# Queueing VectorE's comparisons of the next group ahead of the low half of the weights, in a fused transformer kernel

## The chip, the cores and the metric

The kernel runs on one core of one Trainium2 chip. The metric is the device time of one execution in microseconds (us). Three runs of the kernel before took 1719.59, 1720.41 and 1721.41 us.

## What is computed

The reference is three layers in a row on 256 tokens of width 1024: an attention layer and a gated convolution layer, each with a SwiGLU, and a third layer with a mixer, a cross attention and a mixture of 16384 small experts (PEER). Only that last part matters here. For each token and each of 8 heads it picks 16 experts; expert e = 128 i + j has one row of `u` and one of `v`:

```
s = jnp.einsum('thpc,hpnc->thpn', q, subkeys)
s_top, i_top = lax.top_k(s, PEER_TOPK)
...
experts = jnp.take_along_axis(cand_idx..., pos, axis=-1)
gates = jax.nn.softmax(best, axis=-1)
...
act = jax.nn.gelu(jnp.einsum('cd,ced->ce', xb, u[eb]), approximate=False) * gb
y = jnp.einsum('ce,ced->cd', act, v[eb])
```

The kernel does not gather rows of `u` and `v`. It computes gelu(u x) for all 16384 experts and all 256 tokens, multiplies by a gate that is zero for every expert that a token did not pick, and multiplies by all of `v`.

## The kernel before

**Weights.** A weight stream (class `Stream`) brings all weights in chunks of 1 MB into two raw buffers; SyncE (SP) issues the loads (L215). Each chunk is used in two half chunks. For each of them ScalarE makes a rounded high half `wh` (L231), and VectorE a low half `wl` = raw - wh (L243), and TensorE multiplies three times: high by high, high by low, low by high (L329, L330, L331). There are three buffers each of `wh` and `wl`. The stream works two halves ahead (`look` is 2): the call `w(k)`, which hands out one half, first queues the high and low half of the half chunk two further on. The load that refills a raw buffer is queued behind the second low half of its old chunk.

**The u stage.** The loop `for c in range(NC)` runs over 64 chunks of `u`, with `k` = 0 and 1 for the halves. `proj_stat` gives one half's product u x in 24 matmuls of 256 columns; `gelu` (L1592, L1595) writes it into the tile `big`, which has a column for each of 128 second keys j and 256 tokens, on 128 partitions of first keys i.

**The gates.** For tokens 0 to 127 the gates are written one by one into DRAM by GpSimd (L1491, L1492), loaded back in the v stage (L1534) and multiplied in by GpSimd (L1539). For tokens 128 to 255 they are made in the second part of the u stage, in 32 groups of 4 tokens, which I call the one-hot phase. It is counted in halves e = 2c + k - 91. In half 0 TensorE transposes the selections and ScalarE copies them to `ET` (`hot_T`, L1563, L1564). For group g:

- `hot_make(g)`, on VectorE: one comparison of 512 columns gives the one-hot rows `oi` of the first keys (L1571), four of 128 columns the rows `oj` of the second keys times the gate (L1574). `oi` and `oj` have two slots, g modulo 2.
- `hot_mm(g, J)`: four small matmuls on TensorE give the gates of four tokens in a bank `acc` (L1581); VectorE multiplies them into the columns of `big` that gelu has already written (L1584), and ScalarE copies the rest (L1585) to columns that gelu will meet later. There gelu goes through a buffer `gx`, and a multiply of VectorE or, from group 13 on, of GpSimd (L1596) brings it into `big`; `gated()` queues that one.

In half e the program makes group e-1 and multiplies group e-2.

**What sets the order.** Every engine takes its instructions in the order in which the program writes them; semaphores are placed by the framework from the tiles that are read and written. In half e the code calls, before the change: `w(k)`, the gelu of the chunk before, `proj_stat`, `hot_make(e - 1)`, `gated()`, `hot_mm(e - 2)`.

**The v stage.** Behind the u stage, chunks of `v` are multiplied with `big`, split into high and low parts by `asplit` (ScalarE L361, VectorE L362).

Of the kernel before, what the change touches and what calls it, by code (L numbers as in the profile page):

```python
# [32 lines left out]
HOT0 = 91  # L33
# [230 lines left out]
def body(ctx, tc, I, O):  # L264
# [11 lines left out]
    def bank():  # L276
        return mm.tile([128, 512], F32, name="mm")
# [57 lines left out]
    def proj_stat(ps, w, k, x):  # L335
        w = w(k)
        if FRESH.pop(id(x[0]), None):
            for kt in range(KT):
                a = kt * 128
                for i in range(2):  # L340
                    P.matmul(ps, w[i][:, a:a + 128], x[0][:, kt, :], start=kt + i == 0, stop=False)
            for kt in range(KT):
                a = kt * 128
                P.matmul(ps, w[0][:, a:a + 128], x[1][:, kt, :], start=False, stop=kt == KT - 1)
            return
        for kt in range(KT):
            a = kt * 128
            mm3(ps, w[0][:, a:a + 128], w[1][:, a:a + 128], x[0][:, kt, :], x[1][:, kt, :], kt == 0, kt == KT - 1)
# [582 lines left out]
    for i in range(12):  # L931
        w = W.get(("cv", i))
        for k in range(2):
            c, j = cseq[2 * i + k]
# [294 lines left out]
    for hs in range(8):  # L1229
# [4 lines left out]
        i, k = divmod(hs - 2, 2)  # L1234
# [203 lines left out]
    def pump(b):  # L1438
        credit[0] = min(credit[0] + b, 3.0)
        while RU and credit[0] >= RU[0][0]:  # L1440
            c, f = RU.pop(0)
            credit[0] -= c
            f()
# [92 lines left out]
    def g_mul(c):  # L1536
        if c < NE // 2:
            b = big[:, 2 * c:2 * c + 2, 0:128]
            G.tensor_tensor(b, b, GT.pop(c), op=OP.mult)  # L1539
# [7 lines left out]
    def asplit(j):  # L1547
        if j < NE:
            h, l = AV[j if j < 2 else 2 + j % 4]
            split_to(h, l, big[:, j, :])  # L1550
            AB[j] = (h, l)
# [8 lines left out]
    def hot_T():  # L1560
        ps = bank()
        for i, a in enumerate((0, 1, 3)):
            P.transpose(ps[:, i * 128:i * 128 + 128], slots[:, a, 128:256], ident)  # L1563
        A.activation(ET, ps[:, :384].rearrange("p (a b) -> p a b", a=3), AF.Copy)  # L1564

    def hot_make(g):
        ts = slice(124 - 4 * g, 128 - 4 * g)
        oi, oj = OI[:, g % 2], OJ[:, g % 2]
        io = iota[:, None, :].to_broadcast([128, 4, 128])

        V.tensor_tensor(oi, io, ET[:, 0, ts, None].to_broadcast([128, 4, 128]), op=OP.is_equal)  # L1571
        for i in range(4):
            t = 124 - 4 * g + i
            V.tensor_scalar(oj[:, i, :], iota, ET[:, 1, t:t + 1], ET[:, 2, t:t + 1], op0=OP.is_equal, op1=OP.mult)  # L1574
        HOT[g] = (oi, oj)

    def hot_mm(g, J):
        oi, oj = HOT.pop(g)
        ps = accp.tile([128, 512], F32, name=("acc00", "acc01", "acc10", "acc11")[g % 4])
        for i in range(4):  # L1580
            P.matmul(ps[:, i * 128:i * 128 + 128], oi[:, i, :], oj[:, i, :], start=True, stop=True)  # L1581
        pv = ps.rearrange("p (t j) -> p j t", t=4)
        b = big[:, :, 252 - 4 * g:256 - 4 * g]
        V.tensor_tensor(b[:, :J, :], b[:, :J, :], pv[:, :J, :], op=OP.mult)  # L1584
        A.activation(b[:, J:, :], pv[:, J:, :], AF.Copy)  # L1585
        HB[0] = g + 1

    def gelu(c, ps):
        n = 4 * HB[0]
        p3 = ps.rearrange("p (a b) -> p a b", a=2)  # L1590
        b = big[:, 2 * c:2 * c + 2, :]
        A.activation(b[:, :, :S - n], p3[:, :, :S - n], AF.Gelu)  # L1592
        if n:
            x = bx.tile([128, 2, 128], F32, name="gx", bufs=1)
            A.activation(x[:, :, :n], p3[:, :, S - n:], AF.Gelu)  # L1595
            late.append(lambda: (V if n <= 48 else G).tensor_tensor(b[:, :, S - n:], b[:, :, S - n:], x[:, :, :n], op=OP.mult))  # L1596
# [3 lines left out]
    def gated():  # L1600
        while late:
            late.pop(0)()

    for c in range(NC):
        w = W.get(("u", c))
        ps = bank()
        if 2 * c + 2 >= NE - 32:
            assert not RU
        for k in range(2):
            w(k)  # L1610
            while pend:
                pend.pop(0)()
            if c == NC - 1 and k == 1:
                g_mul(0)
                as0 = bx.tile([128, 4, 256], F32R, name="oi", bufs=1)
                AV += [(as0[:, 0, :], as0[:, 1, :]), (as0[:, 2, :], as0[:, 3, :])]
                asplit(0)
                asplit(1)
            proj_stat(ps[:, k * 256:k * 256 + 256], w, k, xT)
            pump(CRED1)  # L1620
            e = 2 * c + k - HOT0
            if e >= 0:
                assert not RU
            if e == 0:
                hot_T()
            if 1 <= e < 34:
                if e < 33:
                    hot_make(e - 1)
                gated()
                if e > 1:  # L1630
                    hot_mm(e - 2, 2 * c)
            gated()
        pend.append(lambda c=c, ps=ps: gelu(c, ps))
    pend.pop(0)()
    gated()
# [77 lines left out]
```

## Time and profile before

| what | value |
|---|---|
| median of three runs | 1720.41 us |
| the profiled execution | 1723.32 us |
| its span | 1721.5 us |
| granted TensorE clock, mean | 0.992 |
| TensorE (PE) busy | 1656.5 us, 96% |
| VectorE (DVE) busy | 1175.8 us, 68% |
| ScalarE (ACT) busy | 815.0 us, 47% |
| GpSimd (POOL) busy | 483.2 us, 28% |
| DMA, mean | 184 GB/s |

Times within the profile are in us from the start of the span. An engine's busy share is an average over all stages. A row of the timeline gives a start, a duration, the engine, the line of the code, what it writes and reads, and in brackets how long the engine sat idle before it and which instruction ended that. Matmuls are pipelined, so a row of TensorE lasts longer than the step to the next one; the pace is read from the starts.

### The profile page before, as it was taken

The page shows a single profiled execution, that of the slowest core. Times are in us where ns is not written, and L with a number is a line of the kernel's source. Part 1 is how long each engine was busy: PE and PEld are TensorE (multiplying, and loading weights), DVE is VectorE, ACT ScalarE, POOL GpSimd, SP SyncE. Part 2 cuts the span into 40 slices and gives each one's busy share as a digit, 9 for nine tenths or more (in the row PEclk, how much of TensorE's full clock was granted, in tenths as well). Part 3 has the DMA queues.
Part 4 walks back from the last instruction along what each step waited for, and adds up shares of the span by engine and source line. Part 5 has one row for each costly group of instructions (what it writes and reads, how often), then busy time and mean ns, then how long its engine had stood idle before and what let it go on. Part 6 is the DMA issues. An engine that isn't in the chain of part 4 may idle for free.

```text
span 1721.5 us, 27583 instructions
## 1 busy us (share of the span) xinstructions
PE 1656.5 (96%) x11013; PEld 1505.5 (87%) x11013; DVE 1175.8 (68%) x2069; ACT 815.0 (47%) x1260; POOL 483.2 (28%) x446
## 2 busy tenths in 40 slices
PE   8899999999999998998999999999888999999997
PEld 7888999899999977887989999999887888888886
DVE  5897554667654564776558889888777666666665
ACT  5564444434444444564445545445332444444544
POOL 0542000200200022203037887788501211111111
PEclk9999999999999999999999999999999999999999
DMA  7346776455555545434355676766433566666664
GB/s 272 137 140 231 256 237 234 172 208 200 207 182 196 177 166 192 164 104 145 122 193 167 178 196 176 193 181 188 100 121 101 188 219 206 209 219 209 207 217 171
DMA packets 80416, 317.48 MB, mean 184 GB/s; under 512 B 25120, under 2 KB 41760, under 8 KB 45344
## 3 DMA queue, kind: packets, MB, share of 16 engines
q1 hardware_dynamic: 59120, 304.38, 51.7%
q0 software_dynamic: 20736, 10.56, 4.1%
q8 instruction: 86, 1.41, 0.3%
q10 hardware_dynamic: 432, 0.79, 0.1%
q14 instruction: 42, 0.34, 0.1%
HBM read 303.04 MB, written 10.55 MB: 182 GB/s over the span
## 4 chain that ended last, share of the span: by engine, by line
PE 47%; DVE 8%; issue 3%; ACT 3%; POOL 1%; DMA 1%; POOLq 0%; DVEq 0%; ACTq 0%
PE acc L331 8%; PE acc L330 7%; PE acc L329 7%; PE mm L329 7%; PE mm L331 7%; PE mm L330 7%; ACT wh L231 2%; DVE oj L1574 2%; DVE oi L1571 1%; DVE big L1584 1%; DVE wl L243 1%; DMA xTl<-mTl 1%; DVE qkm L1062 1%; POOL wl L243 0%; PE mm L1460 0%
## 5 line engine op out<-in xcount | busy, mean ns | idle before, releaser
L243 DVE TENSOR_TENSOR wl<-raw,wh 128x1024 fp32r<-128x1024 f32 (+1 forms) x511 | 631.5, 1254 | 301.6 <-ACT wh L231 300.3
L231 ACT ACTIVATE wh<-raw 128x1024 fp32r<-128x1024 f32 (+1 forms) x537 | 552.6, 1053 | 377.4 <-PE acc L331 181.7
L329 PE MATMUL mm<-xTh,wh 128*128 128x256 f32 x2328 | 660.2, 284 | 1.1 <-DVE mTl L378 1.1
L331 PE MATMUL mm<-xTh,wl 128*128 128x256 f32 x2328 | 655.8, 282 | 1.8 <-DVE wl L243 1.5
L330 PE MATMUL mm<-xTl,wh 128*128 128x256 f32 x2328 | 655.3, 281 | 0.0
L329 PEld LDWEIGHTS mm<-xTh,wh 128*128 128x128 f32 x2328 | 441.6, 190 | 3.9 <-DVE mTl L378 1.5
L331 PEld LDWEIGHTS mm<-xTh,wl 128*128 128x128 f32 x2328 | 441.3, 190 | 2.7 <-DVE wl L243 1.9
L330 PEld LDWEIGHTS mm<-xTl,wh 128*128 128x128 f32 x2328 | 441.5, 190 | 0.9
L1492 POOL DMA_INDIRECT gd<-slots,idx x128 | 259.9, 2030 | 68.9 <-issue 32.3
L329 PE MATMUL acc<-wh,xTh 128*128 128x512 f32 x632 | 249.7, 395 | 0.0
L330 PE MATMUL acc<-wl,xTh 128*128 128x512 f32 x632 | 249.2, 394 | 0.2 <-DVE wl L243 0.2
L243 POOL TENSOR_TENSOR wl<-raw,wh 128x1024 fp32r<-128x1024 f32 x26 | 64.6, 2491 | 566.8 <-ACT wh L231 565.2
L331 PE MATMUL acc<-wh,xTh 128*128 128x512 f32 x504 | 201.1, 399 | 0.0
L330 PEld LDWEIGHTS acc<-wl,xTh 128*128 128x128 f32 x632 | 119.1, 188 | 30.2 <-DVE wl L243 0.8
L329 PEld LDWEIGHTS acc<-wh,xTh 128*128 128x128 f32 x632 | 119.0, 188 | 28.7 <-issue 0.7
L1539 POOL TENSOR_TENSOR big<-big,oj 128x256 f32<-128x256 f32 x64 | 57.5, 898 | 290.3 <-DMA oj<-gd 290.3
L331 PEld LDWEIGHTS acc<-wh,xTh 128*128 128x128 f32 x504 | 94.6, 188 | 21.7
L880 DVE TENSOR_TENSOR sil<-sil,mm 128x256 f32<-128x256 f32 x44 | 18.5, 421 | 102.7 <-ACT sil L879 102.7
L879 ACT ACTIVATE sil<-mm 128x256 f32<-128x256 f32 x44 | 16.9, 385 | 148.4 <-PE mm L331 148.4
L362 DVE TENSOR_TENSOR xTh<-big,xTh 128x256 fp32r<-128x256 f32 x126 | 79.4, 630 | 0.0
L1491 POOL MEMSET spacer<- 1x1 f32 x128 | 78.9, 616 | 0.0
L330 PE MATMUL acc<-wl,hTh 128*128 128x512 f32 x176 | 69.6, 395 | 0.0
(388 smaller groups left out, 1844.2 us busy)
## 6 DMA issues: line engine op xcount, KB each, us to landing
raw<-in_ws_dram SPq DMA_DIRECT2D x131, 1024.0 KB, 5.1
raw<-in_us_dram SPq DMA_DIRECT2D x64, 1024.0 KB, 5.1
raw<-in_vs_dram SPq DMA_DIRECT2D x64, 1024.0 KB, 4.9
gd<-zt SPq DMA_DIRECT2D x32, 256.0 KB, 6.9
raw<-in_pq_dram SPq DMA_DIRECT2D x8, 1024.0 KB, 4.9
oj<-gd SPq DMA_DIRECT2D x64, 128.0 KB, 4.8
gb<-in_vec_dram POOLq DMA_DIRECT2D x12, 512.0 KB, 7.1
gd<-slots,idx POOLq DMA_INDIRECT x128, 4.0
```

The lines of the kernel that those rows point to most:

```text
L231: self.nc.scalar.activation(h[:, s], self.R[i][:, k * HW:(k + 1) * HW][:, s], AF.Copy)
L243: self.sub[k].tensor_tensor(l[:, s], self.R[i][:, k * HW:(k + 1) * HW][:, s], h.bitcast(F32)[:, s], op=OP.subtract)
L329: P.matmul(ps, lh, rh, start=first, stop=False)
L330: P.matmul(ps, lh, rl, start=False, stop=False)
L331: P.matmul(ps, ll, rh, start=False, stop=last)
L362: V.tensor_tensor(l, src, h.bitcast(F32), op=OP.subtract)
L880: V.tensor_tensor(s, s, pg[:, 256:], op=OP.mult)
L1062: V.scalar_tensor_tensor(y[:, a, :], pad[:, a, j:j + 256], cols[:, 24 + 4 * ft + j:25 + 4 * ft + j], y[:, a, :], op0=OP.mult, op1=OP.add)
L1491: G.memset(spacer, 0.0)
L1492: d = G.indirect_dma_start(out=gd, out_offset=bass.IndirectOffsetOnAxis(ap=idx[:, h, k:k + 1], axis=0), in_=gate[:, 0, h, k:k + 1], in_off ...
L1539: G.tensor_tensor(b, b, GT.pop(c), op=OP.mult)
L1574: V.tensor_scalar(oj[:, i, :], iota, ET[:, 1, t:t + 1], ET[:, 2, t:t + 1], op0=OP.is_equal, op1=OP.mult)
```

## The change

`hot_make(e - 1)` moves from behind `proj_stat` to in front of `w(k)`, so that VectorE's list has the five comparisons ahead of the low half that `w(k)` queues. `hot_mm(e - 2)` stays behind the projection and behind `gated()`, which is now called once.

```
         for k in range(2):
+            e = 2 * c + k - HOT0
+            if 1 <= e < 33:
+                hot_make(e - 1)
             w(k)
             while pend:
                 pend.pop(0)()
...
             proj_stat(ps[:, k * 256:k * 256 + 256], w, k, xT)
             pump(CRED1)
-            e = 2 * c + k - HOT0
             if e >= 0:
                 assert not RU
             if e == 0:
                 hot_T()
-            if 1 <= e < 34:
-                if e < 33:
-                    hot_make(e - 1)
-                gated()
-                if e > 1:
-                    hot_mm(e - 2, 2 * c)
             gated()
+            if 2 <= e < 34:
+                hot_mm(e - 2, 2 * c)
```

VectorE's list in the later part of the one-hot phase, before (`wl` is the low half, `oi` and `oj` are the comparisons, `big<-big,acc` is the multiply of `hot_mm`):

```order
L1584 TENSOR_TENSOR big_8815<-big_8815,acc01_13800 128x110x4
L243 TENSOR_TENSOR wl_13809<-raw_13637,wh_13807 128x1024
L1571 TENSOR_TENSOR oi_9471<-cst_80,ET_9470 128x512
L1574 TENSOR_SCALAR oj_9472<-cst_80,ET_9470 128x128 x4
L1584 TENSOR_TENSOR big_8815<-big_8815,acc10_13842 128x110x4
L243 TENSOR_TENSOR wl_13852<-raw_13724,wh_13850 128x1024
L1571 TENSOR_TENSOR oi_9471<-cst_80,ET_9470 128x512
L1574 TENSOR_SCALAR oj_9472<-cst_80,ET_9470 128x128 x4
L1584 TENSOR_TENSOR big_8815<-big_8815,acc11_13887 128x112x4
```

The same place in the changed kernel:

```order
L1584 TENSOR_TENSOR big_8815<-big_8815,acc01_13800 128x110x4
L1571 TENSOR_TENSOR oi_9471<-cst_80,ET_9470 128x512
L1574 TENSOR_SCALAR oj_9472<-cst_80,ET_9470 128x128 x4
L243 TENSOR_TENSOR wl_13814<-raw_13642,wh_13812 128x1024
L1584 TENSOR_TENSOR big_8815<-big_8815,acc10_13842 128x110x4
L1571 TENSOR_TENSOR oi_9471<-cst_80,ET_9470 128x512
L1574 TENSOR_SCALAR oj_9472<-cst_80,ET_9470 128x128 x4
L243 TENSOR_TENSOR wl_13857<-raw_13729,wh_13855 128x1024
L1584 TENSOR_TENSOR big_8815<-big_8815,acc11_13887 128x112x4
```

Low half and comparisons have changed places; the multiply still ends each half. The lists of the other engines keep their order.

The beginning of the one-hot phase on VectorE, halves 0 to 2, before:

```order
L243 TENSOR_TENSOR wl_12956<-raw_12819,wh_12954 128x1024
L243 TENSOR_TENSOR wl_12992<-raw_12889,wh_12990 128x1024
L1571 TENSOR_TENSOR oi_9471<-cst_80,ET_9470 128x512
L1574 TENSOR_SCALAR oj_9472<-cst_80,ET_9470 128x128 x4
L243 TENSOR_TENSOR wl_13026<-raw_12889,wh_13024 128x1024
L1571 TENSOR_TENSOR oi_9471<-cst_80,ET_9470 128x512
L1574 TENSOR_SCALAR oj_9472<-cst_80,ET_9470 128x128 x4
L1584 TENSOR_TENSOR big_8815<-big_8815,acc00_13059 128x92x4
```

And in the changed kernel:

```order
L243 TENSOR_TENSOR wl_12956<-raw_12819,wh_12954 128x1024
L1571 TENSOR_TENSOR oi_9471<-cst_80,ET_9470 128x512
L1574 TENSOR_SCALAR oj_9472<-cst_80,ET_9470 128x128 x4
L243 TENSOR_TENSOR wl_12997<-raw_12889,wh_12995 128x1024
L1571 TENSOR_TENSOR oi_9471<-cst_80,ET_9470 128x512
L1574 TENSOR_SCALAR oj_9472<-cst_80,ET_9470 128x128 x4
L243 TENSOR_TENSOR wl_13031<-raw_12889,wh_13029 128x1024
L1584 TENSOR_TENSOR big_8815<-big_8815,acc00_13059 128x92x4
```

The first comparisons, which read `ET`, now stand ahead of the low half of half 1.

## Rows read from the trace of the kernel before

**Rows 1.** Busy time by stretch: stretch, us, PE, PEld, DVE, ACT, POOL, clock, DMA share, GB/s
```profile
1200.79:1344.46 143.67, 123.10 (x996) 118.24 (x994) 106.03 (x221) 43.83 (x90) 36.44 (x36) 1.00 0.36 112
...
1354.00:1700.00 346.00, 345.93 (x1483) 278.22 (x1484) 219.64 (x249) 170.55 (x252) 55.60 (x63) 1.00 0.62 213
```

**Rows 2.** Waits from 1200.79 to 1344.46: total us, times, longest
```profile
ACT big L1585 <- DVE big L1584: 98.6, 30, 3.5
...
DVE wl L243 <- ACT wh L231: 37.6, 30, 1.3
...
PE acc L1581 <- DVE oj L1574: 20.4, 27, 1.1
```

**Rows 3.** VectorE in order of time, one turn and the next
```profile
1329.71 0.64 DVE L1584 TENSOR_TENSOR big<-big,acc 128x480 f32<-128x480 f32 x1
1331.56 1.23 DVE L243 TENSOR_TENSOR wl<-raw,wh 128x1024 fp32r<-128x1024 f32 x1 [1.21 <-ACT wh L231]
1332.70 0.69 DVE L1571 TENSOR_TENSOR oi<-cst,ET 128x512 f32<-128x512 f32 x1
1333.30 1.11 DVE L1574 TENSOR_SCALAR oj<-cst,ET 128x128 f32<-128x128 f32 x4
1334.33 0.65 DVE L1584 TENSOR_TENSOR big<-big,acc 128x480 f32<-128x480 f32 x1
...
1337.33 1.17 DVE L1571 TENSOR_TENSOR oi<-cst,ET 128x512 f32<-128x512 f32 x1
...
1339.45 0.65 DVE L1584 TENSOR_TENSOR big<-big,acc 128x488 f32<-128x488 f32 x1
```

**Rows 4.** ScalarE in order of time, the same turn
```profile
1330.38 0.20 ACT L1585 ACTIVATE big<-acc 128x32 f32<-128x32 f32 x1 [3.39 <-DVE big L1584]
1330.47 1.05 ACT L231 ACTIVATE wh<-raw 128x1024 fp32r<-128x1024 f32 x1
```

**Rows 5.** TensorE in order of time: early halves, a waiting product, the halves behind the phase
```profile
1199.99 1.05 PE L1581 MATMUL acc<-oj,oi 128*128 128x128 f32 x8
1200.79 0.36 PE L329 MATMUL mm<-xTh,wh 128*128 128x256 f32 x1
...
1204.50 0.36 PE L329 MATMUL mm<-xTh,wh 128*128 128x256 f32 x1
...
1333.79 1.16 PE L1581 MATMUL acc<-oj,oi 128*128 128x128 f32 x8 [0.61 <-DVE oj L1574]
1334.71 0.37 PE L329 MATMUL mm<-xTh,wh 128*128 128x256 f32 x1
...
1344.46 0.36 PE L329 MATMUL mm<-xTh,wh 128*128 128x256 f32 x1
1344.90 0.28 PE L329 MATMUL mm<-xTh,wh 128*128 128x256 f32 x1
...
1347.39 0.28 PE L329 MATMUL mm<-xTh,wh 128*128 128x256 f32 x1
...
1350.24 0.28 PE L329 MATMUL mm<-xTh,wh 128*128 128x256 f32 x1
```

**Rows 6.** SP's issue, GpSimd's multiply, and loads: KB each, us from issue to landing
```profile
1332.81 0.33 SPq L215 DMA_DIRECT2D raw<-in_us_dram  x1
...
1336.78 1.17 POOL L1596 TENSOR_TENSOR big<-big,gx 128x232 f32<-128x232 f32 x1 [8.57 <-ACT gx L1595]
...
raw<-in_us_dram SPq DMA_DIRECT2D x64, 1024.0 KB, 5.1
```

**Rows 7.** The beginning of the phase: ScalarE and VectorE in order of time
```profile
1194.56 0.49 ACT L1564 ACTIVATE ET<-mm 128x384 f32<-128x384 f32 x1 [2.02 <-PE mm L1563]
...
1196.03 1.22 DVE L243 TENSOR_TENSOR wl<-raw,wh 128x1024 fp32r<-128x1024 f32 x1 [2.23 <-ACT wh L231]
```

**Rows 8.** Entry into the v stage: the split, and TensorE's wait for it
```profile
1353.60 0.72 ACT L361 ACTIVATE oi<-big 128x256 fp32r<-128x256 f32 x2 [2.22 <-POOL big L1539]
...
PE acc L329 <- ACT oi L361: 0.8, 1, 0.8
```

## The prediction

> **What bounds the kernel now.** I read the page first, then busy time by stage, then the waits of the one-hot stage, then that stage in order of time.
>
> The page gives TensorE 96% of the span. By stage [rows 1] that splits: in the stage of the v weights (1354 to 1700) TensorE is busy 345.93 of 346.00 us; in the one-hot stretch ahead of it 123.10 of 143.67. The granted clock is 1.00 in both, the upper of the two levels (2.4 GHz), so the hole is waiting and not a slower clock.
>
> The reader is to see in the waits [rows 2] who starves whom there: TensorE's one-hot products (L1581) waited 27 times for VectorE's comparisons (L1574), 20.4 us; VectorE's low halves (L243) waited 30 times for ScalarE's high halves (L231), 37.6 us; ScalarE's copy (L1585) waited for VectorE's multiply (L1584). TensorE waits for VectorE, VectorE for ScalarE, and ScalarE for VectorE again.
>
> In order of time this is a loop [rows 3, 4]. VectorE's multiply starts at 1329.71 and lasts 0.64. The copy L1585 starts behind it at 1330.38 and the high half at 1330.47 (1.05 us, ScalarE takes its list in order). Only then can the low half run, at 1331.56: VectorE stood idle for 1.21. Low half, comparisons (0.69 and 1.11) and the next multiply follow at 1331.56, 1332.70, 1333.30 and 1334.33. One turn takes 4.62 us, and 5.12 where the first comparison takes 1.17 instead of 0.69 (1334.33 to 1339.45). TensorE's product at 1333.79 starts as VectorE's comparisons come out, with 0.61 of idle ahead of it [rows 5].
>
> TensorE could go faster. At the beginning, before the loop caught up with it, projections start at 1200.79 and 1204.50 [rows 5]: 3.71 us a half. Later matmuls are a touch slower: a projection without products takes 1350.24 - 1347.39 = 2.85, a step of 0.36 for each of its 8 rows of this kind; the first step behind a product is 0.44 (1344.46 to 1344.90), so 0.08 more; a product that did not wait takes 1200.79 - 1199.99 = 0.80. That makes **3.73 us a half**. The stretch from the projection at 1200.79 (half 3) to the one behind the last product (half 34, at 1344.46) holds 31 halves and took 143.67: 4.63 each.
>
> **The change, part by part.**
>
> *Comparisons in front of the low half.* No instruction is added or removed. Right behind the multiply VectorE now has five comparisons whose inputs are all old: they start at once and take 1.63 (1332.70 to 1334.33). ScalarE meanwhile does its copy and high half, which end 1.21 behind the multiply. So the wait of 1.21 is covered by 1.63 of work, and the low half starts without idle time. VectorE's own half is then the sum of its starts: low half 1.14 (1331.56 to 1332.70), comparisons 1.63, multiply 0.64: 3.41; with the long first comparison 0.48 more, 3.89, in every second half of the later part, so 3.65 on average. On average that is inside TensorE's 3.73. TensorE becomes what sets the half, and VectorE waits for it in front of the multiply.
>
> The gain: 31 x 3.73 = 115.6 against 143.67: about **28.0 us**. With the early 3.71 it is 28.7; if VectorE needed 3.89 in every half it would be 143.67 - 120.6 = 23.1. I take 28.0, since the two nearest sums (3.73 of TensorE, 3.65 of VectorE) put TensorE in front.
>
> *Two slots.* The comparisons overwrite the slot of two groups earlier, which a product of TensorE has read. In the new list the multiply of that same group stands directly ahead of them and already waits for that product, so this adds nothing.
>
> *The low half comes later in its half,* by 1.63. Who waits: TensorE's third matmul of the projection two halves later. The low half ends about 0.64 + 1.63 + 1.23 = 3.50 behind a product, and is used two halves (7.46) behind it: 4.0 of slack. Nothing.
>
> *SP's queue.* Every second low half frees a weight buffer, and SP issues the next load at that moment (1332.81, right behind the low half that began at 1331.56) [rows 3, 6]. It is needed by a high half three halves later. In the new order that leaves about 3 x 3.73 less the 2.86 from the multiply's end to the low half's, 8.3 us; a load lands 5.1 us after its issue [rows 6]. Nothing; 3.2 of cover.
>
> *GpSimd's queue.* Its multiply (L1596) is the neighbour of the long comparison [rows 3, 6]: it began at 1336.78, while VectorE was in the low half, and the comparison at 1337.33 took 1.17. In the new order it meets the low half and the multiply. I leave its 0.48 on VectorE.
> The Trainium skill, page "SBUF — State Buffer", section "SBUF: two separate sides", says that GpSimd and a VectorE operation with two SBUF inputs take a shared port pair in turn, each for a whole instruction; the long comparison agrees (1.17 against 0.69). By that rule the multiply, which reads one input from PSUM, would not queue there, and VectorE's half would be 3.41 throughout: the sum is the same, and the first rival below less likely.
>
> *The first half.* The first comparisons now wait for ScalarE's transposed selections (L1564, 1194.56 to 1195.05) and the low half behind them moves from 1196.03 to about 1196.7 [rows 7]; it has two halves of lead. Nothing, at worst 0.7.
>
> *The end.* Where TensorE enters the v weights it waits 0.8 for the first split of the activations [rows 8]. That chain (load of the gates, GpSimd's multiply, ScalarE's split at 1353.60) hangs on ScalarE and GpSimd work that ran late behind VectorE; with VectorE on time I expect the 0.8 to go. Ends: 0 and 0.8; I take 0.8, as three projections (3 x 2.85 = 8.5) lie between the last product, behind which the code lets that load go out, and the v weights, and a load lands some 5 us after its issue [rows 6].
>
> **The sum.** 28.0 + 0.8 = 28.8 us off the profiled execution's 1723.3 (its span of 1721.5 and 1.8 around it): 1694.5. The median of the runs is 1720.41, 2.9 lower, so **1691.6**. The v stage behind is all TensorE [rows 1] and hands the gain through undiminished.
>
> **The rivals.**
> 1. *VectorE stays the bound.* If GpSimd's neighbour costs its 0.48 in each half and not each second, VectorE needs 3.89 and the half is that: 23.1 us, with the end's 0.8 1696.5. For it: 3.65 against 3.73 is close. Against: GpSimd has one such multiply per two halves, and none in the first twelve groups. It decides where VectorE's mean half passes 3.73. Chance 0.09.
> 2. *Only the wait comes back.* The 20.4 us of the row go, and the slower pace of the product (0.92 at 1333.79 against 0.80) and the overlap that the row doesn't count stay: 1700.0. Against: the early halves show 3.71 as a whole. Chance 0.04.
> 3. *Nothing changes.* The comparisons cannot start behind the multiply since they wait for something that I took for old (their slot, a semaphore); VectorE idles there instead: 1720. Chance 0.03.
> 4. *Slower: TensorE waits for the low halves.* The low half is now last before the multiply. If the two halves of lead were not there, each projection would stop at its third matmul for the comparisons in front: 32 x 1.63 = 52 us, 1772. It decides when VectorE lags by over 4.0 us; before, VectorE lagged too, and no row shows a projection waiting for a low half [rows 2]. Chance 0.03.
>
> **How the numbers follow.** Forecast 0.81 (1691.6; 1690.9 to 1692.4 by the two values of the half and the two of the end). The low end allows the early 3.71 and a run 1 us faster: 1689.5. The high end takes in the first rival without the end's 0.8: 1697.5. About 0.1 is left out. A measurement tells about 0.2% (3.4 us) from no change. Faster: 0.81 + 0.09 + 0.04 = 0.94; same 0.03; slower 0.03.
>
> **What would show it.** Right: in the same 31 halves products start every 3.7 us (stretch about 116 us); the rows "DVE wl waits for ACT wh" (37.6) and "PE acc waits for DVE oj" (20.4) are gone or below 3 us; instead VectorE's multiply waits for L1581, a tenth to four tenths of a us a half. VectorE's busy time is as before. Wrong: any wait of a projection for wl (rival 4); idle time of VectorE in front of L1571 (rival 3); products still waiting for the comparisons with VectorE never idle (rival 1); a load of weights that a high half waits for.

## The result and the profile after

| kernel | median, us | runs | ratio to before | 95% interval |
|---|---|---|---|---|
| before | 1720.0 | 4 | 1 | |
| changed | 1690.57 (1688.28 to 1692.74) | 4 | 0.983 | 0.9813 to 0.9847 |

The change saves 29.4 us of the median; 28.8 were forecast, and 1690.57 lies in the range. The two profiled executions differ by more, 1723.3 against 1690.0, that is by 33.3.

Where the time went is read from the same 31 halves as before, from the projection behind the first product to the one behind the last. Busy time by stretch in the changed kernel, columns as in [rows 1]:

```profile
1197.56:1312.47 114.91, 114.91 (x996) 114.91 (x994) 103.53 (x218) 45.58 (x94) 33.54 (x35) 1.00 0.47 146
1321.00:1667.00 346.00, 346.00 (x1485) 278.38 (x1484) 220.16 (x248) 170.00 (x250) 55.81 (x63) 1.00 0.62 212
```

143.67 us have become 114.91, 28.8 less, and TensorE is busy in all of it. The v stage behind is as full as before. Of the 33.3 us between the two profiled executions 3.2 lie ahead of the phase: the first product comes at 1196.75, before at 1199.99 [rows 5]. The change touches nothing there, and the runs of one kernel are spread over some 4 us.

The waits in that stretch of the changed kernel (total us, times, longest):

```profile
ACT big L1585 <- DVE big L1584: 59.0, 26, 2.9
DVE big L1584 <- PE acc L1581: 10.0, 31, 0.4
...
DVE wl L243 <- ACT wh L231: 1.2, 1, 1.2
```

Against [rows 2]: the low half's wait of 37.6 us has gone but for one time (the last low half, which has no comparisons in front), the products' wait of 20.4 has gone altogether, and a new one stands in their place, VectorE's multiply waiting for the product 31 times, 0.3 us each. It costs nothing: it is VectorE that waits for the engine that sets the pace.

VectorE of the changed kernel in order of time, one half of the later part and the start of the next, and ScalarE below it:

```profile
1297.99 0.65 DVE L1584 TENSOR_TENSOR big<-big,acc 128x480 f32<-128x480 f32 x1 [0.37 <-PE acc L1581]
1298.56 0.68 DVE L1571 TENSOR_TENSOR oi<-cst,ET 128x512 f32<-128x512 f32 x1
1299.16 1.11 DVE L1574 TENSOR_SCALAR oj<-cst,ET 128x128 f32<-128x128 f32 x4
1300.19 1.22 DVE L243 TENSOR_TENSOR wl<-raw,wh 128x1024 fp32r<-128x1024 f32 x1
1301.63 0.65 DVE L1584 TENSOR_TENSOR big<-big,acc 128x480 f32<-128x480 f32 x1 [0.22 <-PE acc L1581]
...
1298.68 0.20 ACT L1585 ACTIVATE big<-acc 128x32 f32<-128x32 f32 x1 [2.08 <-DVE big L1584]
1298.77 1.05 ACT L231 ACTIVATE wh<-raw 128x1024 fp32r<-128x1024 f32 x1
```

The copy and the high half are done at 1299.82; the comparisons in front last until the low half starts at 1300.19. In [rows 3] VectorE was idle in that place. This turn takes 3.64, the one before it 3.78, and the mean is 3.71; in [rows 3] it is 4.62 and more.

TensorE of the changed kernel, around the last product and at the entry into the v stage:

```profile
1311.66 1.05 PE L1581 MATMUL acc<-oj,oi 128*128 128x128 f32 x8
1312.47 0.36 PE L329 MATMUL mm<-xTh,wh 128*128 128x256 f32 x1
...
1321.00 0.40 PE L329 MATMUL acc<-wh,oi 128*128 128x512 f32 x1
```

The product takes 0.81 and waits for nothing (0.92, with 0.61 of idle ahead, in [rows 5]), and the v stage begins 8.53 behind 1312.47, the bare length of three projections; the wait of 0.8 [rows 8] is gone.

GpSimd's multiply between VectorE's low half and multiply in the changed kernel, and below it the first comparison of the phase:

```profile
1303.83 1.22 DVE L243 TENSOR_TENSOR wl<-raw,wh 128x1024 fp32r<-128x1024 f32 x1
1304.09 1.50 POOL L1596 TENSOR_TENSOR big<-big,gx 128x232 f32<-128x232 f32 x1 [5.95 <-ACT gx L1595]
1305.40 0.66 DVE L1584 TENSOR_TENSOR big<-big,acc 128x488 f32<-128x488 f32 x1 [0.36 <-PE acc L1581]
...
1191.78 0.69 DVE L1571 TENSOR_TENSOR oi<-cst,ET 128x512 f32<-128x512 f32 x1 [1.29 <-ACT ET L1564]
```

GpSimd needs 1.50 for the size that took 1.17 in [rows 6], and VectorE's long comparison is 0.68 or 0.69 everywhere. The first comparison waits 1.29 for the transposed selections [rows 7]; nobody waits for it.

### The profile page after: what moved, and what is told of

It reads as the page before. It is cut to its first block, busy times and chain, and to the rows that moved or that the text cites. A ratio compares the mean times of both kernels' runs of the same rounds, so it can differ in the third digit from the quotient of the medians.

```text
span 1688.2 us, 27583 instructions
## 1 busy us (share of the span) xinstructions
PE 1644.9 (97%) x11013; PEld 1499.3 (89%) x11013; DVE 1172.8 (69%) x2069; ACT 814.9 (48%) x1260; POOL 478.5 (28%) x446
## 4 chain that ended last, share of the span: by engine, by line
PE 55%; DVE 3%; issue 1%; DMA 1%; ACT 1%; POOL 1%; POOLq 0%; DVEq 0%; ACTq 0%; SPq 0%
PE mm L329 9%; PE mm L331 9%; PE mm L330 9%; PE acc L330 8%; PE acc L329 8%; PE acc L331 7%; PE acc L1581 2%; DMA xTl<-mTl 1%; DVE qkm L1062 1%; POOL wl L243 0%; PE mm L1460 0%; PE mm L1336 0%; PE mm L1303 0%; DVE wl L243 0%; DVE r L453 0%
## 5 line engine op out<-in xcount | busy, mean ns | idle before, releaser
L1492 POOL DMA_INDIRECT gd<-slots,idx x128 | 253.0, 1977 | 68.9 <-issue 32.0
L1539 POOL TENSOR_TENSOR big<-big,oj 128x256 f32<-128x256 f32 x64 | 56.8, 888 | 289.8 <-DMA oj<-gd 289.8
```

Source lines behind the costliest of these rows:

```text
L1492: d = G.indirect_dma_start(out=gd, out_offset=bass.IndirectOffsetOnAxis(ap=idx[:, h, k:k + 1], axis=0), in_=gate[:, 0, h, k:k + 1], in_off ...
```

## The experiments

The theory is the loop of the prediction: multiply, copy, high half, low half, comparisons, multiply. Work in front of the low half covers the wait of 1.21; TensorE then sets the half. The time of the 31 halves in each run's profile tells more than the medians, which carry the spread ahead of the phase.

| run | median, us | ratio (95% interval) | 31 halves, us |
|---|---|---|---|
| changed | 1690.57 | 0.983 (0.9813 to 0.9847) | 114.91 |
| e1_first_only | 1699.79 | 0.9877 (0.986 to 0.9893) | 123.99 |
| e2_copy_later | 1691.51 | 0.9826 (0.981 to 0.9842) | 114.90 |
| e3_plus_short | 1690.19 | 0.9826 (0.9809 to 0.9842) | 114.90 |
| e4_plus_long | 1696.77 | 0.9864 (0.9847 to 0.988) | 118.11 |
| e5_lead_one | 1692.47 | 0.9839 (0.9822 to 0.9855) | 114.91 |
| e6_no_lead | 1858.52 | 1.0792 (1.0773 to 1.081) | 280.29 |
| e7_both | 1689.85 | 0.9827 (0.9811 to 0.9843) | 114.91 |
| e8_products_single | 1676.02 | 0.9736 (0.9716 to 0.9756) | 101.07 |

**Half of the change (e1).** The one long comparison stays in front, the four short ones go back.

```
         V.tensor_tensor(oi, io, ET[:, 0, ts, None].to_broadcast([128, 4, 128]), op=OP.is_equal)
+        HOT[g] = (oi, oj)
+
+    def hot_make_j(g):
+        oi, oj = HOT[g]
         for i in range(4):
...
+            if 1 <= e < 33:
+                hot_make_j(e - 1)
             gated()
```

> Changed kernel, but only the first comparison of a group (128x512, L1571) stands in front of the low half; the four of 128x128 go back behind the projection. Theory (the loop multiply, copy, high half, low half, comparisons; whatever stands in front of the low half covers the 1.21 us wait for the high half): 0.60 of the 1.21 are covered, the half is 4.63 - 0.60 = 4.03, the 31 halves about 125 us, the time about 1720 - 19 = 1701. Rival that only the lateness of the comparisons against TensorE's products counts: the last of them come out where they came before, 1720. Rival that the gain is VectorE and GpSimd out of each other's way (1.17 against 0.69 in ten rows, some 3.5 us in all): 1716.

124.0 us, 1699.8. VectorE of this run (L1578 is the four comparisons, L1587 the multiply):

```profile
1276.31 0.61 DVE L1587 TENSOR_TENSOR big<-big,acc 128x440 f32<-128x440 f32 x1
1276.83 0.69 DVE L1571 TENSOR_TENSOR oi<-cst,ET 128x512 f32<-128x512 f32 x1
1278.16 1.23 DVE L243 TENSOR_TENSOR wl<-raw,wh 128x1024 fp32r<-128x1024 f32 x1 [0.64 <-ACT wh L231]
1279.31 1.31 DVE L1578 TENSOR_SCALAR oj<-cst,ET 128x128 f32<-128x128 f32 x4
1280.54 0.60 DVE L1587 TENSOR_TENSOR big<-big,acc 128x448 f32<-128x448 f32 x1
```

0.64 us of idle time is left of 1.21: the cover works to the length of what stands there. Both rivals fall. The short comparisons come out behind the low half as before, and two thirds of the gain are there (19.7 of 28.8 us in the stretch). GpSimd's neighbour still lengthens a comparison (1.31 against 1.11 in the halves between), so it isn't that.

**The same loop cut elsewhere (e2).** The order of before, but ScalarE's copy is queued behind the next high half.

```
-        A.activation(b[:, J:, :], pv[:, J:, :], AF.Copy)
+        copies.append(lambda: A.activation(b[:, J:, :], pv[:, J:, :], AF.Copy))
...
             w(k)
+            while copies:
+                copies.pop(0)()
```

> Kernel before (comparisons behind the low half), with ScalarE's copy L1585 queued behind the next half's high half instead of ahead of it. Theory: this cuts the same loop at ScalarE, the high half no longer waits for the multiply, VectorE's idle 1.21 goes though no comparison is moved; VectorE needs 3.41 to 3.89, mean 3.65, TensorE 3.71: the 31 halves take 115 to 118 us, the time 1690 to 1694. Rival that the place of the comparisons itself is what counts (VectorE against GpSimd, or the products): about 1720, at best 1716.

114.90 us, as in the changed kernel, with no comparison moved. VectorE and, behind the dots, ScalarE of this run:

```profile
1274.90 0.62 DVE L1584 TENSOR_TENSOR big<-big,acc 128x448 f32<-128x448 f32 x1 [0.24 <-PE acc L1581]
1275.44 1.22 DVE L243 TENSOR_TENSOR wl<-raw,wh 128x1024 fp32r<-128x1024 f32 x1
1276.58 1.04 DVE L1571 TENSOR_TENSOR oi<-cst,ET 128x512 f32<-128x512 f32 x1
...
1273.95 1.06 ACT L231 ACTIVATE wh<-raw 128x1024 fp32r<-128x1024 f32 x1 [1.80 <-PE mm L330]
1275.56 0.22 ACT L1585 ACTIVATE big<-acc 128x64 f32<-128x64 f32 x1 [0.56 <-DVE big L1584]
```

The high half now waits for TensorE to free its buffer (1.80) and is done before the multiply ends (1275.01 against 1275.52), so the low half follows the multiply at once. The long comparison beside GpSimd's multiply (1.04 against 0.68) is still there, and the half is TensorE's all the same. What counted was the loop and not the place of the comparisons in itself.

**Both cuts (e7).** The edit of e2, made to the changed kernel.

> Changed kernel, with ScalarE's copy L1585 also queued behind the next high half. Theory (TensorE sets the half, the loop is covered already): the same as the changed kernel, 1689 to 1692. If a rest of the loop still costs: below 1688.

114.91 us: the second cut finds nothing left.

**How much VectorE has left (e3, e4).** One comparison is done twice, a short one in e3 and the long one in e4. The line that e4 adds at the end of `hot_make` (e3 repeats the one of `oj[:, 0, :]`):

```
+        V.tensor_tensor(oi, io, ET[:, 0, ts, None].to_broadcast([128, 4, 128]), op=OP.is_equal)
```

> Changed kernel, with one of the four 128x128 comparisons of each group done twice (0.26 us more of VectorE in each half, same result). Theory (0.33 a half of VectorE is left over): it fits, 1690.6 to 1692. Rival that VectorE is the bound: 31 x 0.26 = +8: 1699.

114.90 us: 0.26 a half fit into VectorE's 0.33. The multiply's waits for the product fall from 31 to 3.

> Changed kernel, with the 128x512 comparison of each group done twice (0.60 us more of VectorE in each half, same result). Theory (TensorE sets the half at 3.71, VectorE has the 0.33 a half left that its multiply waits for the product): 0.27 a half over 31 halves comes out, +8.4: 1699. Rival that VectorE is the bound: the whole 0.60, +18.6: 1709. If neither: 1690.6.

118.11 us in the stretch, 3.2 more and not 8.4. Busy time by stretch in this run:

```profile
1198.78:1316.89 118.11, 118.11 (x996) 116.47 (x994) 118.11 (x248) 43.88 (x90) 40.01 (x34) 1.00 0.42 134
```

And TensorE at the entry into the v stage, in order of time:

```profile
1327.12 0.50 PE L329 MATMUL acc<-wh,oi 128*128 128x512 f32 x1 [1.22 <-ACT oi L361]
```

VectorE is busy for all of the stretch, 0.19 us a half slower than TensorE (3.90 between two multiplies against 3.71), which would be 5.9 over 31 halves. But TensorE feels it only once VectorE has used up its lead: products start 3.71 apart for the first 15 halves, and 3.8 to 3.9 apart only from there on. In addition the wait at the entry is back (the v stage begins 10.23 behind the last product's projection, not 8.53). 3.2 and 1.7 make 4.9 of the 6.2 us between the medians; the rest is within their spread. My 8.4 forgot the lead and took VectorE's half 0.08 too long.

**The lead of the weights (e5, e6).** In e5 the lead is 1, in e6 it is 0:

```
+            W.look = 1 if 1 <= e < 33 else 2
             if 1 <= e < 33:
                 hot_make(e - 1)
             w(k)
```

> Changed kernel, with the lead of the weight stream set from two halves to one in the halves with comparisons. By the prediction's count the low half is done 3.5 us behind a product and would be needed 3.71 + 0.25 = 3.96 behind it: 0.46 left, 1690.6 to 1692. If the slack of 4.0 us that the prediction gave is over by more than that, projections wait: each 0.1 us missing costs 3 us.

114.91 us: in the stretch one half of lead is enough, and the 0.46 that I counted holds at least in sign. The median of 1692.47 lies above the 1692 that I gave as the upper end, and part of it is no spread. The v stage begins 9.76 behind the last product's projection in this run, 1.2 more than in the changed kernel:

```profile
1320.06 1.41 DVE L243 TENSOR_TENSOR wl<-raw,wh 128x1024 fp32r<-128x1024 f32 x1 [0.27 <-ACT wh L231]
1320.35 1.70 POOL L1539 TENSOR_TENSOR big<-big,oj 128x256 f32<-128x256 f32 x1
```

GpSimd's first multiply by the loaded gates (L1539) meets a low half of VectorE here and takes 1.70; what that does is told below, under "The end".

> Changed kernel, with the lead of the weight stream set from two halves to none in the halves with comparisons. This prices the fourth rival of the prediction. Theory (the low half's new place is free because of the lead): each projection stops until multiply 0.65, comparisons 1.63 and low half 1.23 are done behind a product, then 2.6 of projection and 0.8 of product follow: 6.9 a half, 31 halves 214 us, the time about 1790. If the lead isn't what makes it free: 1691.

280 us and 1858.5: much more than the 214 and 1790. Busy time by stretch in this run:

```profile
1202.74:1483.03 280.29, 190.42 (x992) 178.23 (x993) 103.92 (x216) 46.14 (x94) 33.72 (x33) 0.74 0.19 60
```

And one half of TensorE in order of time, with rows of the same kinds left out:

```profile
1265.24 0.39 PE L329 MATMUL mm<-xTh,wh 128*128 128x256 f32 x1 [1.90 <-ACT wh L231]
1265.47 0.28 PE L330 MATMUL mm<-xTl,wh 128*128 128x256 f32 x1
1266.77 0.58 PE L331 MATMUL mm<-xTh,wl 128*128 128x256 f32 x1 [1.02 <-DVE wl L243]
...
1268.00 0.41 PE L330 MATMUL mm<-xTl,wh 128*128 128x256 f32 x1
1268.21 0.41 PE L331 MATMUL mm<-xTh,wl 128*128 128x256 f32 x1
...
1270.06 0.28 PE L329 MATMUL mm<-xTh,wh 128*128 128x256 f32 x1
1270.18 0.28 PE L330 MATMUL mm<-xTl,wh 128*128 128x256 f32 x1
...
1270.78 0.94 PE L1581 MATMUL acc<-oj,oi 128*128 128x128 f32 x7
```

The chain is the expected one: each projection stops for the high half and again for the low half. What I had not counted is TensorE's clock. Its mean in the stretch is 0.74, a mix of the two levels: behind the gap the matmuls step by 0.21 us (1268.00 to 1268.21), later in the same half by 0.12 (1270.06 to 1270.18). The projection from its third matmul to the product takes 4.0 us in place of 2.6. On average over the halves that piece takes 4.3 (2.6 in the changed kernel), the piece from the product to VectorE's multiply 1.4 (1.1; I had counted 0.8), and VectorE's piece between them 3.4, against 3.5 expected. So the 2.1 us above 6.9 lie in TensorE's pieces.

**TensorE as the bound (e8).** The one-hot tiles in the weights' format.

```
-    OI = bx.tile([128, 2, 4, 128], F32, name="oi", bufs=1)
-    OJ = bx.tile([128, 2, 4, 128], F32, name="oj", bufs=1)
+    OI = bx.tile([128, 2, 4, 128], F32R, name="oi", bufs=1)
+    OJ = bx.tile([128, 2, 4, 128], F32R, name="oj", bufs=1)
```

> Changed kernel, with the one-hot tiles oi and oj in the format of the weights' high halves (fp32r) instead of fp32, so that the gates of tokens 128 to 255 are rounded to that format; the lists of all engines stay as they are. Theory (TensorE sets the half of 3.71): a product then takes at most four steps of the 0.118 us that a 128x256 matmul of that format takes, 0.24 to 0.47 instead of 0.80, and TensorE's half 3.17 to 3.40; VectorE's own half, 3.71 less the 0.33 that its multiply waits, is 3.38 and sets the pace: 31 x 0.33 = 10 us less, 1680. If the half is set by anything but TensorE's products and projections: 1690.6.

101.07 us, 14.6 below the changed kernel in the median: this version beats both, at the price of the rounded gates. TensorE's last product and the next projection, and VectorE of this run:

```profile
1299.64 0.56 PE L1581 MATMUL acc<-oj,oi 128*128 128x128 f32 x4
1300.04 0.33 PE L329 MATMUL mm<-xTh,wh 128*128 128x256 f32 x1
...
1274.83 0.68 DVE L1584 TENSOR_TENSOR big<-big,acc 128x464 f32<-128x464 f32 x1
1275.38 0.73 DVE L1571 TENSOR_TENSOR oi<-cst,ET 128x512 fp32r<-128x512 f32 x1
1275.98 1.16 DVE L1574 TENSOR_SCALAR oj<-cst,ET 128x128 fp32r<-128x128 f32 x4
1277.01 1.26 DVE L243 TENSOR_TENSOR wl<-raw,wh 128x1024 fp32r<-128x1024 f32 x1
1278.14 0.68 DVE L1584 TENSOR_TENSOR big<-big,acc 128x464 f32<-128x464 f32 x1
```

A product takes 0.40 in place of 0.81, the half falls to 101.07 / 31 = 3.26, and no wait of the multiply for a product is left in this run. So TensorE did set the half in the changed kernel. VectorE's half is 3.31 between these multiplies, not the 3.38 that I expected, and its lead carries the difference: products start 3.26 apart to the end. Hence 13.8 in the stretch and not 10.

## Why the prediction was right

- **What bounds the kernel.** The loop through VectorE and ScalarE held: cutting it at either engine (the change, e2) gives the same 114.9 us, 0.57 of cover takes 0.57 off the wait and the turn from 4.63 to 4.00 (e1), two cuts give no more than one (e7).
- **The cover.** 1.63 of comparisons over 1.21 of copy and high half: the low half starts with no idle time.
- **The gain of the stretch.** Forecast 28.0 from TensorE's 3.73 a half; measured 28.8, since a half takes 114.91 / 31 = 3.71. The later step of 0.356 us between like matmuls, from which I took 3.73, did not come back: it is 0.352 throughout the changed stretch, though 0.356 ahead of the phase in both kernels. Why the two steps differ by one per cent isn't settled. That 28.8 is also the sum that was forecast for the whole is chance: from the first projection of the stretch to the v stage the two traces differ by 29.8, 28.8 here and 1.1 at the end.
- **VectorE's half.** I gave 3.41, with GpSimd 3.65. The starts in e4 and e8 show 3.30 (3.90 less the 0.60 added; 3.31): I had added the multiply's whole duration where the next instruction starts 0.1 earlier. And GpSimd's 0.48 went from VectorE altogether: the long comparison takes 0.68 in all 32 groups, and GpSimd's multiply takes up the time itself, 1.50 against 1.17 for the same size. By the Trainium skill, page "SBUF — State Buffer", section "SBUF: two separate sides", GpSimd and a VectorE operation with two SBUF inputs take turns. The trace agrees: GpSimd's multiply begins 0.26 behind the start of the low half (two SBUF inputs) and ends 0.54 behind its end, and VectorE's multiply, which reads one of its inputs from PSUM, is not lengthened beside it (0.66). VectorE is busy for 103.53 us of the stretch, where I had expected the 106.03 of before; the lengthened comparisons made up 3.2 of those. So the first rival, VectorE as the bound, was further away than its 0.09. In e2 the comparison is still lengthened in every second half of the later part, and TensorE sets the half even so. The rival put 0.48 on every half, and no run does just that, but e4 puts 0.60 on every half and loses 3.2 in the stretch, less than the 4.9 (28.0 less 23.1) that the rival asked for.
- **The other rivals.** "Only the wait comes back" fell with the 28.8. "Nothing changes" fell: VectorE is not idle before any comparison but the very first (1.29, for the transposed selections, the wait foreseen for the first half). "Slower" was right in what it hung on, the lead of the weights (e6). Its price of 52 us over the kernel before was too low: without any lead in these halves the changed kernel takes 138 more than the kernel before, and 168 more than with its lead. What the kernel before would take without the lead was not run.
- **Things costed at nothing.** Low halves (e5: in the stretch still free with one half of lead), SP's loads, the two slots: no row of the changed kernel shows a wait for them.
- **The end.** The 0.8 went, as forecast; the v stage begins 8.53 behind the last product's projection, and began 1354.07 - 1344.46 = 9.61 behind it before, so the end gave 1.1. The reason was half right. GpSimd's multiply by the loaded gates, the link ahead of the split, before, with VectorE's low halves beside it and TensorE's first matmul of the v stage; the last row is the same multiply in the changed kernel:

```profile
1350.08 2.89 DVE L243 TENSOR_TENSOR wl<-raw,wh 128x1024 fp32r<-128x1024 f32 x2
...
1351.86 1.71 POOL L1539 TENSOR_TENSOR big<-big,oj 128x256 f32<-128x256 f32 x1
...
1354.07 0.50 PE L329 MATMUL acc<-wh,oi 128*128 128x512 f32 x1 [0.82 <-ACT oi L361]
...
1318.37 0.74 POOL L1539 TENSOR_TENSOR big<-big,oj 128x256 f32<-128x256 f32 x1
```

  It starts 7.4 behind the last product's projection before and 5.9 in the changed kernel: that is the lateness which the prediction named. But it also takes 0.97 longer before, where a low half of VectorE runs beside it, and this the prediction did not have. The first part of the changed kernel's split is done some 1.4 before TensorE needs it (1319.63 against 1321.00), so the lateness of 1.5 alone would have cost about 0.1, an estimate from these rows. Over all ten traces the two go together: with 0.74 the v stage begins 8.5 behind the last product's projection (changed, e2, e3, e6, e7, e8), with 1.70 or 1.71 it begins 9.6 to 10.2 behind it (before, e1, e4, e5). In e5 VectorE is on time in the stretch and the wait is back, so "VectorE on time" was not enough for it.

## What to carry to other kernels

Where several engines wait for each other in a ring, add up one turn before looking for the slow engine: here none was slow, and the turn of 4.6 us hid a TensorE half of 3.7. An instruction whose inputs are old belongs in front of one that waits for another engine, and is worth the smaller of its own length and that wait, until the next engine's pace is reached. An engine that is a few per cent too slow for its stage does no harm until its lead is used up, so price a delay by rate, number of turns and lead together.

## What was not expected of the hardware

- TensorE's granted clock. With gaps of 0.6 to 1.1 us in 27 of the halves it stayed at 1.00 in the stretch of before [rows 1, 2]. In e6, with two gaps in each half, 1.90 and 1.02 in the one shown, it went to and fro between the two levels, 0.74 on average; the matmul's step was 0.21 at the lower one against 0.118, and the half took 280.29 / 31 = 9.0 us where 6.9 had been worked out at the upper level.
- GpSimd and VectorE beside each other. A multiply of GpSimd (128x256) took 0.74 with VectorE idle and 1.71 beside a low half, and its wait shows as duration, not as idle time in front. At the entry into the v stage that was worth more than the lateness it came with.
- VectorE's durations with no idle time anywhere (e8): the comparison of 128x512 reads 0.73 against 0.68, the low half 1.26 against 1.22, while the starts stand no further apart (0.60 and 1.13). In such a stretch only the starts tell the pace.
